# Placing the projection of a pair's gated half ahead of its recurrence

## The chip, the cores and the metric

The kernel runs on one core of a Trainium2 chip. The metric is the device time of one execution in microseconds (us), as the median of several runs. Engine names are those of the profile: PE is TensorE's matmul, PEld its weight load, DVE is VectorE, ACT is ScalarE, POOL is GpSimd, SP is SyncE, which here only issues DMAs.

## The reference, cut to what matters

One layer of a hybrid decoder over 544 tokens: 512 of a prompt and 8 sequences of 4 sample tokens. The part around the change:

```python
xn = rms_norm(x, norm1_g)
proj = xn @ w_in                              # 2048 -> 5 * 1024 + 288 columns
z_a = gelu(proj[..., :2 * W_A])               # u and v of the gated half, 1024 columns each
y_a = u * (spatial mixing of layer_norm(v))   # group A
y_b = rwkv7_mix(proj[..., 2 * W_A:], ...)     # group B: r, k, v, a recurrence over time per head
h = x + concat([y_a, y_b]) @ w_out
```

After it come the expert retrieval (`peer_ffn`) and a final norm, which take the larger part of the time and which the change doesn't touch.

## The kernel before, in words

Everything is kept transposed: a tile has 128 features as partitions and the tokens along its free axis. `front` computes the layer up to the gated half's share of the output projection, `back` the rest. All projections are float32 products done as three matmuls on split operands (`hi*xh + hi*xl + lo*xh`).

`project` (L160) computes one tile of 128 columns of `w_in` for all 552 token columns: two halves of 276 columns, each 16 x 3 = 48 matmuls (L171) into a PSUM tile of pool `pg` (two buffers). Its weights come through `weights` (L148): four DMAs of 256 KB into `wr` (four buffers), a cast on ACT (L155, `wh`) and a difference on DVE (L156, `wl`), in pools of seven buffers.

After the `v` side of the gated half, whose mixed result goes to a DRAM scratch `mix`, and three projections for the low-rank parts, a loop over eight pairs of heads (L544) does for pair p:

- `shifted` (L242) three times, for r, k and v: a projection, its eviction on DVE (L249) into a tile `p` (two buffers), and the token shift on DVE (L251, L252, L254) into a tile `r`, `k` or `v` (two buffers each).
- a DMA of the pair's low-rank weights `lora` (L547), and `seg` (L280) three times: tokens 0 to 255, 256 to 511, and the sample tokens. A `seg` begins with a chain over ACT, DVE and POOL from its first products (L300, L301 on `xwa` and `lora`, L323 on the squares of the scaled k) to the matrices `AR`, `BK`, `E`, goes on to a triangular inverse by doubling (L419, L434 to L441), and ends with the chunk recurrence (L466 to L501) and a normalisation (L508 to L525) whose result goes to the scratch `yT` rows 8 to 15. The second `seg` needs the state of the first.
- `utile` (L529): one more projection, for u of the gated half. Its two halves are evicted on DVE (L535) into a tile `p`, go through Gelu on ACT (L536), are multiplied with the mixed tile `mxr` (loaded by L538, one buffer; L539, L541), and go to `yT` rows 0 to 7 (L542). Nothing in it reads what a `seg` wrote, and no `seg` reads what it wrote.

After the loop `xns.close()` gives the memory of the projections' operands `xh`, `xl` free, and the stage `ya`, whose tiles take that memory, loads `yT` rows 0 to 7 (L559), splits them (L560, L561 into `yh`, `yl`) and multiplies them with the upper half of `w_out`: 16 x 48 = 768 matmuls (L573). When the pools of `front` close, `back` begins with the lower half of `w_out` (L675).

The order of the work on each engine is not written by hand. A planner runs when the program is built: it keeps its own model of when instructions become ready, and for each engine takes, among those ready in its model, the one with the lowest number in program order. `tc.high_priority(offset=n)` lowers the number by n (3000 for the weights, 2000 for the evictions). The order found is then fixed, and each engine runs its queue in that order. So work later in the program is placed into an engine's gaps of work earlier in the program.

Of the kernel before, what the change touches and what calls it, by code (L numbers as in the profile page):

```python
# [67 lines left out]
def front(tc, I, O, SC, dbg=None):  # L68
# [13 lines left out]
    def P(n, i=0, w=1):  # L82
        o = _PAR[n] + i
        return par[:, o:o + w]
# [75 lines left out]
    def project(ti, M=128, pool=None):  # L160
        pool, tag = pool or (pg, "g")
        ws = [weights(I["w_in"][ti], 4 * q, 4) for q in range(4)]
        out = []
        for h in range(2):
            ps = pool.tile([128, 512], F32, name=tag)
            c = slice(h * HC, h * HC + HC)
            n = 0
            for k in range(KT):
                hi, lo = (w[:, k % 4, :M] for w in ws[k // 4])
                for a, b in ((hi, xh), (hi, xl), (lo, xh)):  # L170
                    T.matmul(ps[:M, :HC], a, b[:, k, c], start=n == 0, stop=n == 3 * KT - 1)  # L171
                    n += 1
            out.append(ps[:M, :HC])
        return out
# [67 lines left out]
    def shifted(ti, n, name, M=128, bufs=None):  # L242

        ps = project(ti, M)
        p = b0.tile([128, CW], F32, name="p", bufs=2)
        for h in range(2):
            c = slice(h * HC, h * HC + HC)
            with tc.high_priority(offset=EV):
                V.tensor_mul(p[:M, c], ps[h], rs[:M, c])  # L249
        d = b0.tile([128, CW], F32, name="d")  # L250
        V.tensor_sub(d[:M, 1:], p[:M, :CW - 1], p[:M, 1:])  # L251
        V.tensor_scalar(d[:M, 0:1], p[:M, 0:1], -1.0, None, op0=OP.mult)  # L252
        q = b0.tile([128, CW], F32, name=name, bufs=bufs)
        V.scalar_tensor_tensor(q[:M], d[:M], P("mu", n)[:M], p[:M], op0=OP.mult, op1=OP.add)  # L254
        return q
# [273 lines left out]
    def utile(h):  # L529
        ps = project(h)  # L530
        u = b0.tile([128, CW], F32, name="p", bufs=2)
        for i in range(2):
            c = slice(i * HC, i * HC + HC)
            with tc.high_priority(offset=EV):
                V.tensor_mul(u[:, c], ps[i], rs[:, c])  # L535
            A.activation(u[:, c], u[:, c], AF.Gelu)  # L536
        mx = bw.tile([128, TC], F32, name="mxr")
        S.dma_start(mx, SC["mix"][h])  # L538
        V.tensor_mul(mx[:, :TP], mx[:, :TP], u[:, :TP])  # L539
        ms = mx[:, TP:].rearrange("p (b t) -> p b t", t=4)  # L540
        V.tensor_mul(ms, ms, u[:, TP:].rearrange("p (b t) -> p b t", t=5)[:, :, 1:])  # L541
        G.dma_start(SC["yT"][h], mx)  # L542

    for p in range(NPAIR):  # L544
        q = [shifted(16 + 8 * i + p, 8 * i + p, "rkv"[i], bufs=2) for i in range(3)]
        lora = bw.tile([128, 4, 128], F32, name="lora", bufs=2)
        S.dma_start(lora, I["lora"][p])  # L547
        st = seg(p, 0, q, lora, None)
        st = seg(p, 1, q, lora, st)
        seg(p, 2, q, lora, None)  # L550
        utile(p)
    xns.close()

    with tc.tile_pool(name="ya", bufs=1, side="right", reuse_waits="tile") as ya:
# [577 lines left out]
def emit(tc, I, O):  # L1132
    with tc.tile_pool(name="dram", bufs=1, space=DRAM) as dr:
        SC = scratch(dr)
        front(tc, I, O, SC)
        back(tc, I, O, SC)
# [87 lines left out]
```

## Time and profile before

| | |
|---|---|
| median of 3 runs | 4056.84 us (4054.25 to 4058.28) |
| the profiled execution | 4046.83 us, its span 4044.7 us |
| PE busy in the span | 3632.6 us, 90% |
| PEld, DVE, ACT, POOL busy | 84%, 76%, 35%, 32% |
| mean granted TensorE clock | 0.958 of 2.4 GHz |
| the pair loop | from about 235 to about 1063 us of the span |
| the stage `ya` | its matmuls from 993 to 1143 us, beside the last pair up to 1063 us |

Matmuls overlap in the array, and a row's duration is that of one from its start to its modelled end; the distance between starts in an unbroken stream is what one costs. Busy time of PE is therefore near 100% wherever matmuls follow one another closely, whatever their kind.

### The profile page before, as it was taken

What the parts mean: (1) busy time and instruction counts of PE and PEld (TensorE: products, weight loads), DVE (VectorE), ACT (ScalarE), POOL (GpSimd) and SP (SyncE); (2) the same over time, 40 slices, a digit from 0 to 9 for tenths busy, and PEclk for the clock granted to TensorE, in tenths of its full rate; (3) what the DMA queues carried; (4) which work ended last, traced back from release to release, by engine and by line L of the source; (5) the groups of instructions that cost most, each with busy time, mean ns of one, the idle gap of its engine ahead of it and who ended that gap; (6) DMA issues with size and microseconds to landing.
All of it is one profiled execution on the core that took longest, in us unless ns stands there. A gap on an engine that the chain in (4) does not pass through costs nothing.

```text
span 4044.7 us, 65633 instructions
## 1 busy us (share of the span) xinstructions
PE 3632.6 (90%) x25519; PEld 3413.5 (84%) x25519; DVE 3084.6 (76%) x5034; ACT 1425.5 (35%) x2501; POOL 1282.9 (32%) x1190
## 2 busy tenths in 40 slices
PE   8999999999999998889988888888988888898997
PEld 8888888887898997889888778887978788888997
DVE  4566666666645579999957888888898888888995
ACT  4244444444333232227942222222222222223233
POOL 1212222222143002221134443444434443444453
PEclk9999999999999999999999989999999998999998
DMA  4211111112554236667677898889889888998983
GB/s 156 102 62 56 58 59 57 59 57 78 178 170 120 75 115 234 235 225 260 252 242 287 311 341 310 318 310 341 317 326 325 317 322 305 333 331 311 358 332 123
DMA packets 252822, 886.53 MB, mean 219 GB/s; under 512 B 26920, under 2 KB 84008, under 8 KB 200480
## 3 DMA queue, kind: packets, MB, share of 16 engines
q1 hardware_dynamic: 184672, 423.77, 31.5%
q0 software_dynamic: 67840, 458.57, 30.3%
q8 instruction: 201, 3.29, 0.3%
q14 instruction: 109, 0.89, 0.1%
HBM read 823.47 MB, written 58.76 MB: 218 GB/s over the span
## 4 chain that ended last, share of the span: by engine, by line
PE 47%; DVE 16%; issue 15%; DMA 12%; POOL 8%; ACT 1%; SPq 0%; DVEq 0%; POOLq 0%; ACTq 0%
PE g L171 10%; PE o L1071 9%; PE g L675 9%; DMA row<-in_v_tab,idx 4%; PE q L970 4%; DVE wl L662 4%; DMA row<-in_u_tab,idx 3%; POOL row L807 3%; PE i L419 2%; DVE row L819 2%; DMA wr<-in_vT 2%; PE g L573 2%; POOL ac L1055 2%; POOL cl L1059 2%; DMA wr<-in_uT 1%
## 5 line engine op out<-in xcount | busy, mean ns | idle before, releaser
L661 ACT CAST wh<-wr 128x1024 fp32r<-128x1024 f32 x560 | 585.7, 1049 | 1441.4 <-PE o L1071 540.5
L662 DVE TENSOR_TENSOR wl<-wr,wh 128x1024 fp32r<-128x1024 f32 x560 | 730.3, 1308 | 205.2 <-ACT wh L661 200.4
L1071 PE MATMUL o<-ch,wh 128*128 128x352 f32 x2048 | 688.3, 343 | 190.1 <-DVE y L1079 146.8
L675 PE MATMUL g<-xh,wh 128*128 128x352 f32 x2048 | 678.3, 331 | 70.0 <-DVE ac L768 59.0
L1071 PE MATMUL o<-cl,wh 128*128 128x352 f32 x2048 | 695.0, 340 | 41.7 <-POOL cl L1059 41.7
L1071 PE MATMUL o<-ch,wl 128*128 128x352 f32 x2048 | 687.2, 337 | 0.7 <-DVE wl L662 0.7
L675 PE MATMUL g<-xh,wl 128*128 128x352 f32 x2048 | 672.9, 329 | 3.5 <-DVE wl L662 3.5
L675 PE MATMUL g<-xl,wh 128*128 128x352 f32 x2048 | 671.8, 328 | 0.0
L1071 PEld LDWEIGHTS o<-ch,wh 128*128 128x128 f32 x2048 | 407.5, 200 | 218.1 <-DVE y L1079 80.5
L819 DVE SCALAR_TENSOR_TENSOR row<-row,xrow 128x2048 f32<-128x2048 f32 x192 | 457.2, 2382 | 92.1 <-DMA row<-in_u_tab,idx 90.8
L838 DVE SCALAR_TENSOR_TENSOR acc<-row,dots,acc 128x2048 f32<-128x2048 f32 x186 | 458.8, 2467 | 63.7 <-DMA row<-in_v_tab,idx 61.6
L807 POOL DMA_INDIRECT row<-in_u_tab,idx x192 | 291.0, 1516 | 618.1 <-DVE y L1079 259.1
L675 PEld LDWEIGHTS g<-xh,wh 128*128 128x128 f32 x2048 | 391.4, 191 | 81.8 <-issue 40.9
L1071 PEld LDWEIGHTS o<-cl,wh 128*128 128x128 f32 x2048 | 411.2, 201 | 49.2 <-POOL cl L1059 49.0
L807 POOL DMA_INDIRECT row<-in_v_tab,idx x192 | 264.7, 1379 | 572.1 <-DVE y L1079 341.6
L1071 PEld LDWEIGHTS o<-ch,wl 128*128 128x128 f32 x2048 | 409.8, 200 | 1.0 <-DVE wl L662 1.0
L675 PEld LDWEIGHTS g<-xh,wl 128*128 128x128 f32 x2048 | 392.0, 191 | 5.6 <-DVE wl L662 5.4
L675 PEld LDWEIGHTS g<-xl,wh 128*128 128x128 f32 x2048 | 393.0, 192 | 1.0 <-issue 1.0
L171 PE MATMUL g<-xh,wh 128*128 128x276 f32 x1248 | 379.3, 304 | 9.6 <-ACT xh L113 9.6
L171 PE MATMUL g<-xl,wh 128*128 128x276 f32 x1248 | 375.9, 301 | 0.2 <-DVE xl L114 0.2
L171 PE MATMUL g<-xh,wl 128*128 128x276 f32 x1248 | 374.6, 300 | 0.0
L1079 DVE TENSOR_TENSOR y<-o,y 128x352 f32<-128x352 f32 x496 | 238.7, 513 | 36.0 <-PE o L1071 36.0
(636 smaller groups left out, 6378.6 us busy)
## 6 DMA issues: line engine op xcount, KB each, us to landing
wr<-in_uT SPq DMA_DIRECT2D x256, 512.0 KB
wr<-in_vT SPq DMA_DIRECT2D x256, 512.0 KB
wr<-in_w_in SPq DMA_DIRECT2D x172, 256.0 KB
Gd<-st POOLq DMA_DIRECT2D x11, 2048.0 KB
gl<-Gd SPq DMA_DIRECT2D x32, 704.0 KB
wr<-in_w_q SPq DMA_DIRECT2D x32, 512.0 KB
Cd<-ac POOLq DMA_DIRECT2D x52, 176.0 KB
ac<-Cd SPq DMA_DIRECT2D x52, 176.0 KB
```

The costliest lines, as they stand in the source:

```text
L171: T.matmul(ps[:M, :HC], a, b[:, k, c], start=n == 0, stop=n == 3 * KT - 1)
L419: return halves(lambda o, c, h: T.matmul(o, a[hs[h], c], b[hs[h], c], start=True, stop=True))
L573: T.matmul(ps[:, :TC // 2], a, b[:, k, h * TC // 2:(h + 1) * TC // 2], start=n == 0, stop=n == 23)
L661: A.copy(hi, raw)
L662: V.tensor_sub(lo, raw, hi)
L675: T.matmul(ps[:, :N], a, b[:, k, c], start=n == 0, stop=n == 3 * KT - 1)
L807: d = G.indirect_dma_start(out=u, out_offset=None, in_=tab, in_offset=bass.IndirectOffsetOnAxis(ap=idx[w][:, r:r + 1], axis=0))
L819: i = V.scalar_tensor_tensor(u, u, 1.0, xrow, op0=OP.mult, op1=OP.mult, accum_out=dots[w][:, r:r + 1])
L838: i = V.scalar_tensor_tensor(acc, u, dots[w][:, r:r + 1], acc, op0=OP.mult, op1=OP.add)
L970: T.matmul(ps[c][:, :TQ], w[:, j:j + 128], x, **e)
L1071: T.matmul(ps[j][:, :TD], a, x_, start=i + n == 0, stop=i == GB - 1 and n == 2)
L1079: last = V.tensor_add(yT[:, m], ps[j][:, :TD], prev)
```

## The change

In the loop over the pairs, the call of `utile(p)` moves from behind the three calls of `seg` to a place between the `shifted` calls and the load of `lora`. No instruction is added or removed; their numbers in program order change, and with them what the planner may put ahead of what.

```diff
     for p in range(NPAIR):
         q = [shifted(16 + 8 * i + p, 8 * i + p, "rkv"[i], bufs=2) for i in range(3)]
+        utile(p)
         lora = bw.tile([128, 4, 128], F32, name="lora", bufs=2)
         S.dma_start(lora, I["lora"][p])
         st = seg(p, 0, q, lora, None)
         st = seg(p, 1, q, lora, st)
         seg(p, 2, q, lora, None)
-        utile(p)
     xns.close()
```

## Rows read from the trace of the kernel before

**Rows 1.** From the page: busy tenths of PE and granted clock in 40 slices of 101 us each.

```profile
PE   8999999999999998889988888888988888898997
PEclk9999999999999999999999989999999998999998
```

**Rows 2.** Busy time in stretches of 104.2 us, one pair each (start and end, length; then the busy us and count of instructions of PE, PEld, DVE, ACT, POOL; the granted clock; DMA share, GB/s).

```profile
342.50:446.70 104.20, 101.84 (x1044) 86.79 (x1042) 71.19 (x191) 46.22 (x107) 23.58 (x43) 1.00 0.17 58
655.10:759.30 104.20, 101.80 (x1044) 86.77 (x1042) 71.17 (x191) 46.20 (x107) 23.58 (x43) 1.00 0.17 58
863.50:967.70 104.20, 101.80 (x1043) 86.77 (x1043) 71.15 (x191) 46.22 (x107) 23.60 (x44) 1.00 0.17 55
```

**Rows 3.** The stretches of one pair's period, all work; columns as in rows 2.

```profile
645.40:651.70 6.30, 6.30 (x51) 6.30 (x51) 3.81 (x10) 2.15 (x4) 1.08 (x2) 1.00 0.54 174
651.70:677.00 25.30, 22.93 (x220) 20.30 (x218) 19.36 (x39) 19.77 (x40) 9.45 (x15) 1.00 0.18 62
677.00:699.70 22.70, 22.70 (x311) 19.16 (x306) 15.19 (x49) 10.40 (x28) 8.17 (x14) 1.00 0.13 40
699.70:745.40 45.70, 45.67 (x455) 38.38 (x452) 30.88 (x90) 13.67 (x34) 4.90 (x12) 1.00 0.15 52
```

**Rows 4.** The same stretches, the projections' matmuls (L171) alone: busy us and count of PE and PEld, clock, DMA.

```profile
645.40:651.70 6.30, 6.30 (x50) 6.26 (x50) 1.00 0.54 174
651.70:677.00 25.30, 14.76 (x100) 12.86 (x98) 1.00 0.18 62
677.00:699.70 22.70, 9.98 (x55) 7.58 (x55) 1.00 0.13 40
699.70:745.40 45.70, 29.36 (x172) 23.21 (x172) 1.00 0.15 52
```

**Rows 5.** The timeline of PE in an unbroken stretch of projection (start us, duration, operation).

```profile
646.24 0.29 PE L171 MATMUL g<-xh,wl 128*128 128x276 f32 x1
646.37 0.29 PE L171 MATMUL g<-xh,wh 128*128 128x276 f32 x1
646.50 0.29 PE L171 MATMUL g<-xl,wh 128*128 128x276 f32 x1
```

**Rows 6.** Who PE waited for from 651.7 to 677 us (us in total, times, longest us).

```profile
PE q L379 <- DVE BK L350: 1.0, 1, 1.0
PE i L419 <- DVE Ti L429: 0.6, 1, 0.6
PE i L419 <- DVE Ti L438: 0.6, 1, 0.6
PE q L402 <- DVE E L393: 0.2, 1, 0.2
```

**Rows 7.** The timeline at the start of a pair's first `seg`: ACT, and below the line of dots DVE; in brackets the idle time before and its releaser.

```profile
651.80 0.62 ACT L155 CAST wh<-wr 128x512 fp32r<-128x512 f32 x1 [0.91 <-PE g L171]
652.44 1.28 ACT L303 ACT_TABLE_LOAD   x1
653.73 0.47 ACT L303 ACTIVATE sw<-q,hb 128x256 f32<-128x256 f32 x1
660.74 1.28 ACT L536 ACT_TABLE_LOAD   x1
662.03 0.43 ACT L536 ACTIVATE p<-p 128x276 f32<-128x276 f32 x1
666.69 0.47 ACT L303 ACTIVATE sw<-q,hb 128x256 f32<-128x256 f32 x1 [0.37 <-PE q L301]
...
651.93 0.44 DVE L249 TENSOR_TENSOR p<-g,rs 128x276 f32<-128x276 f32 x1 [0.31 <-PE g L171]
653.06 0.72 DVE L251 TENSOR_TENSOR d<-p 128x551 f32<-128x551 f32 x1
654.04 0.78 DVE L254 SCALAR_TENSOR_TENSOR v<-d,par,p 128x552 f32<-128x552 f32 x1
654.74 0.28 DVE L306 TENSOR_SCALAR sw<-sw 128x256 f32<-128x256 f32 x1
```

**Rows 8.** The line of the load of `mxr` in one period, on the SP queue: its wait (an event) and the DMA (count, duration in ns as minimum, median and maximum, first and last start).

```profile
L538 SPq EVENT_SEMAPHORE  x1: 6592/6592/6592, 678.0 to 678.0; - x1
L538 SPq DMA_DIRECT2D mxr<-mix x1: 327/327/327, 684.6 to 684.6; - x1
```

**Rows 9.** The last pair and the stage `ya`: stretches, all work; columns as in rows 2.

```profile
964.40:976.60 12.20, 11.16 (x87) 10.44 (x86) 8.45 (x17) 11.41 (x24) 3.20 (x6) 1.00 0.20 64
976.60:988.70 12.10, 10.78 (x118) 9.02 (x115) 9.98 (x21) 7.62 (x14) 6.21 (x8) 1.00 0.17 46
988.70:1001.50 12.80, 9.59 (x130) 7.61 (x128) 8.93 (x19) 7.98 (x20) 3.03 (x5) 0.87 0.68 216
1021.50:1063.00 41.50, 40.90 (x366) 32.64 (x367) 27.19 (x82) 9.01 (x24) 5.11 (x12) 1.00 0.28 81
1105.00:1143.60 38.60, 38.60 (x309) 38.60 (x309) 11.02 (x27) 4.34 (x7) 3.23 (x6) 1.00 0.43 139
```

**Rows 10.** The matmuls of `ya` (L573) alone in the stretches of the last pair: busy us and count of PE and PEld, clock, DMA.

```profile
988.70:1001.50 12.80, 1.19 (x5) 0.72 (x5) 0.87 0.68 216
1001.50:1021.50 20.00, 9.12 (x39) 5.75 (x39) 1.00 0.20 57
1021.50:1063.00 41.50, 23.35 (x134) 18.17 (x135) 1.00 0.28 81
```

**Rows 11.** The timeline around the first work of `ya`: the last matmul on `xh` and `xl`, the first load of `yT`, the first matmul of `ya`, the last split of its operand.

```profile
988.69 0.29 PE L171 MATMUL g<-xh,wl 128*128 128x276 f32 x1
988.88 0.33 SPq L559 DMA_DIRECT2D yr<-yT  x1
992.96 0.39 PE L573 MATMUL g<-yh,wh 128*128 128x272 f32 x1 [1.22 <-ACT yh L560]
1021.56 0.71 DVE L561 TENSOR_TENSOR yl<-yr,yh 128x544 fp32r<-128x544 f32 x1
```

## The prediction, made before the change was run

> **What bounds the kernel now.** I read the page's slices first [rows 1]: PE is busy in 80 to 90% of every slice and its clock is near full, so the loop over the pairs (about 235 to 1063 us) is to be read as work on PE. The second view is busy time by period [rows 2]: the reader is to see that each pair takes the same 104.2 us, that PE is busy for 101.8 of them, and that DVE (71), ACT (46) and POOL (24) are not near. PE's true idle time is only 104.2 - 101.8 = 2.4 us in a pair. The third view cuts one period into stretches and counts the projections' matmuls in each [rows 3, 4]. From 645.4 to 651.7 us PE does 50 of them and nothing else: the recurrence of the previous pair is over, and that of this one cannot start, since its v is still being projected. From 651.7 to 677 us the first `seg` of the pair goes through its chain on ACT, DVE and POOL, and 100 projection matmuls fill PE beside it. These are the pair's own `utile` (96 matmuls), the only projection that stands next in program order, and a few more. From 677 to 745.4 us the inverse and the recurrence have PE's gaps, and 55 + 172 projection matmuls of the next pair go into them. Then PE is alone with the rest of that pair's v again.
>
> A projection matmul costs 0.127 us in an unbroken stream [rows 5], so a projection of 96 costs 12.2 us, and the four of a pair 48.7 us: half of the period. The other half is the small matmuls and the switching between the two kinds. The short stretch in which PE does projections alone says that the filler is never used up within a pair: the recurrence hides what it can, and 6.3 us stay over.
>
> **The change part by part.** Nothing is added or removed; four things move.
>
> First, the order of the projections. Before it is r, k, v, [seg], u, r, k, v, [seg], u. After it is r, k, v, u, [seg], r, k, v, u, [seg]. The chain of projections is the same, and between two recurrences there are still four of them: u of this pair and r, k, v of the next before, r, k, v and u of the next after. `seg` keeps its precedence over all of those behind it. As filler one matmul is worth another, and I find no resource that would keep u of the next pair out of the gaps: it needs a `pg` and a `p` buffer, which turn over at each eviction, and weights, which come in the same order as before. So I expect the 50 lone matmuls to become matmuls of u instead of v, and the period to stay. Cost: 0, covered by the other pair's recurrence. If that cover were gone, all of u would stand alone, 12.2 us in each pair (a rival below).
>
> Second, what goes ahead of a `seg`'s chain on DVE and ACT. Before, the eviction and shift of v (0.44 + 0.72 + 0.78 us on DVE) and the table load for Tanh (1.28 us) stand between the last projection matmul at 651.7 and the chain; L303 starts 2.0 us behind it [rows 7]. After, v is long done, and the eviction (0.44) and Gelu (0.43) of u's second half stand there. Gelu and this Tanh do not need separate loads: behind a Gelu the Tanh at 666.69 started without one [rows 7]. So L303 could start some 0.23 + 0.44 + 0.43 + 0.1 = 1.2 us behind the last matmul, 0.8 earlier. This can only take from the 2.4 us of waits in that stretch [rows 6], which begin with 1.0 us before L379. The bounds: 2.4 us gained in a pair, if all of the waits go; 0.8 us lost, if Gelu's table load lands in front of the chain (1.28 less 0.44). I take a quarter of the 0.8, 0.2 us gained, because the order on PE was fixed by a model which will also see the chain begin earlier and put fewer matmuls ahead of L379. Eight pairs: -1.6 us (bounds -19 and +6).
>
> On what is left to gain the Trainium skill speaks in "Perfetto Trace Analysis", section Identifying the Most-Contended Engine: matmul busy time is no good measure of how close TensorE is to its limit, weight-load busy time is better. Here weight loads fill 86.8 of 104.2 us of a pair, against 6.30 of 6.30 in the lone stretch [rows 2, 3]; by that measure 17 us of a pair are in play and not 2.4. I don't price these 17: they are the changeovers between small and large matmuls, and their number goes with the gaps of the recurrence, which the change leaves.
>
> Third, DMAs and queues. u's load of `mxr` waits at the head of the SP queue for the single buffer, 6.6 us in a pair [rows 8], and the weight loads and `lora` wait behind it. It will still do so once in a pair, about 12 us earlier or later against the recurrence. The store L542 on POOL goes with it. PE never waits for weights in this stretch [rows 6], since up to seven buffers stand ready. Cost 0; if weights did run out, it would be up to those 6.6 us in a pair, which I hold for unlikely with DMA at 17% [rows 2].
>
> Fourth, the last pair, where the symmetry ends. Before, u of pair 7 is the filler of the last chain (964.4 to 988.7 us); with its last matmul the memory is free, the loads of `ya` start 0.2 us later, and its first matmul comes 4.3 us after that [rows 11]. After, u comes before the chain, ends 12.2 us behind v, and the last `seg` starts that much later with only `ya` as filler. The 12.2 us of u in front are compensated by the 12.2 us no longer spent in the chain only as far as `ya` fills the hole. `ya` ramps slowly, because its operand is split at low precedence: in the first 33 us only 5 + 39 of its matmuls run, 5.6 us [rows 10, 11]. I let the same 44 run in the new hole: 12.2 - 5.6 = 6.6 us stay open. Against it, the operand of `ya` is then complete about when the recurrence proper begins, and the 12.80 - 9.59 = 3.2 us of idle PE that the start of `ya` causes now [rows 9] go. Together +3.4 us. Bounds: if nothing fills the hole and the clock falls as it does at the start of `ya` now, 12.2 + 1.7 = +13.9; if the hole is filled and idle time and clock are both gained, -4.9. The 1.7: a clock of 0.87 over 12.8 us [rows 9] is 3.3 us at 1.2 GHz, in which half the work is lost. Behind this, `ya` runs alone until 1143 us [rows 9], so a delay or a gain up to there goes to the end in full, and `seg` itself, over at 1063, has 80 us to spare.
>
> The sum: 0 - 1.6 + 0 + 3.4 = +1.8 us. On the profiled execution's 4046.83 us that is 4048.6; the median of the runs lies 10 us higher (0.25%), so I add to the median: 4056.84 + 1.8 = 4058.6 us. What this kernel's measurement can tell from no change is about 0.2%, 8 us.
>
> **The rivals.** *Faster: the chain becomes shorter.* If the waits of the chain vanish in most pairs, the gain is 1.2 to 2.4 us in each, 10 to 19 us, and with the last pair at its sum 4041 to 4050 us. For it: the ACT queue is the fullest there (19.8 of 25.3 us, [rows 3]), and two table loads of u leave it. It decides from 1.5 us in a pair. Against: the order on PE is fixed beforehand. The Trainium skill, "ScalarE: Activation LUTs", section What ACT_TABLE_LOAD costs, would make this larger: 1.28 us of load and 1.38 us of drain for each switch. The trace shows the 1.28 and no drain behind it: the Gelu starts 0.01 us after its load [rows 7], so the measured price stands.
>
> *Slower: the hole in the last pair stays open.* +9 to +14 us, 4066 to 4071 us. For it: the slow ramp of `ya` and a granted clock that already falls to 0.87 there. It decides where less than a quarter of the hole is filled and the idle time at `ya`'s start returns. The Trainium skill, "TensorE: Matmul & The Clock Gate", part 1, names the mechanism: the slow clock is the default and activity releases it. The stretch from 988.7 us, PE idle for 3.2 us, agrees [rows 9].
>
> *Slower in every pair: u stands alone.* If the planner does not reach u of the next pair while the recurrence has gaps (a `p` buffer held while L538 waits, for instance), u costs its 12.2 us in each of seven pairs: +85 us, 4142 us. A twelfth of that would already show. Against it: 227 matmuls go into 677 to 745.4 us now, across three projections and their buffers [rows 4].
>
> **How the numbers follow.** Forecast within 8 us of before: 0.52. Shorter chain: 0.20. Hole in the last pair: 0.20. u alone, in whole or part: 0.08. So faster 0.20, same 0.52, slower 0.28. The range reaches from the middle of the faster rival's (4040) to past the hole with some loss in the pairs added (4056.84 + 13.9 + 6 = 4077, to 4080); the +85 is left out.
>
> **What would show it.** Right: periods of 103.5 to 104.7 us, with about 50 lone matmuls of u ahead of L300 and r and k of the next pair as filler of the chain; L303 without a table load; the last u ending some 12 us before its old distance to the end of the last `seg`; PE idle for 5 to 9 us more in the 25 us behind it. Wrong: a period that moves by more than 1 us, a lone stretch much above 6 us, PE waiting for `wl` or `wh`, or a stage behind 1143 us whose length changes by itself.

## The result, and the profile after

The changed kernel takes 4090.29 us (median of 4 runs, 4087.22 to 4102.47), the kernel before 4057.56 us beside it. The ratio is 1.0087, with a 95% interval of 1.0066 to 1.0109: slower, by 33 us where 2 were forecast, and above the range, which ended at 4080 us. The profiled execution is the slowest of the four (4102.47 us, span 4100.8), and that of before lay 10 us under its median, so the two profiles stand further apart (55.6 us) than the medians. 8 us of this lie ahead of the pair loop, in code that is the same in both: the first L300 comes at 254.7 us after 234.6 before, and only 12.2 us of that are the u which now stands in front. A kernel below with the same start of the loop reaches that L300 at 247.5 us, so these 8 us are spread between executions.

The first page line to look at is that of the slices. They tell nothing here, since PE looks as busy as before [rows 1]:

```profile
PE   8899999999899998889988788888888887989997
PEclk9999999999899999999999999999999999899998
```

The loss shows as soon as busy time is cut by period, as in [rows 2] (start and end, length; then busy us and count of PE, PEld, DVE, ACT, POOL; granted clock; DMA share, GB/s). A pair takes 109.20 us where it took 104.2, and each pair is like the next. The instructions are the same but for table loads on ACT, 9 in a pair where there were 11:

```profile
345.50:454.70 109.20, 105.18 (x1048) 88.35 (x1045) 73.27 (x191) 43.99 (x104) 23.70 (x42) 1.00 0.16 55
563.20:672.40 109.20, 105.18 (x1044) 88.36 (x1043) 73.26 (x190) 43.99 (x104) 23.71 (x42) 1.00 0.16 55
672.40:781.60 109.20, 105.18 (x1044) 88.35 (x1043) 73.28 (x190) 43.99 (x104) 23.71 (x42) 1.00 0.17 55
```

Seven periods of 5.0 us make 35 us, the whole loss of the median. PE's busy time grew from 101.8 to 105.2 us for the same matmuls, at full clock, so it counts waits too: a wait shorter than the modelled tail of the matmul ahead of it is not seen as idle. Weight-load busy time grew by 1.6 us only; by it 20.85 us of a pair are open (without a weight load) now, after 17.42.

So the cut has to follow the work. These are the stretches of one pair, the projections' matmuls (L171) alone (columns: PE, PEld, clock, DMA; a matmul that lies across a border is counted on both sides, so the sums below go by starts). They run from the first L300 to the first L379, to the first L469 (the recurrence begins), to the first L451 (the third `seg`'s state), to the last L519, and to the next L300. First the kernel before:

```profile
651.70:661.80 10.10, 8.01 (x59) 7.40 (x57) 1.00 0.22 76
661.80:688.90 27.10, 11.43 (x70) 9.35 (x70) 1.00 0.19 62
688.90:737.90 49.00, 29.13 (x164) 22.27 (x163) 1.00 0.13 42
737.90:749.30 11.40, 7.18 (x44) 5.87 (x44) 1.00 0.10 36
749.30:755.90 6.60, 6.40 (x50) 6.41 (x50) 1.00 0.49 168
```

and the changed kernel:

```profile
693.60:705.40 11.80, 9.04 (x70) 8.67 (x68) 1.00 0.29 102
705.40:732.70 27.30, 9.05 (x52) 7.12 (x52) 1.00 0.12 41
732.70:781.50 48.80, 26.98 (x145) 19.91 (x144) 1.00 0.10 32
781.50:794.40 12.90, 8.70 (x56) 7.40 (x56) 1.00 0.21 71
794.40:802.80 8.40, 8.16 (x64) 8.16 (x64) 1.00 0.43 134
```

The second and third stretch, the inverse and the recurrence, last 76.1 us in both. In them stand 70 + 163 = 233 projection matmuls before and 52 + 144 = 196 after. 37 fewer at 0.127 us are 4.7 us of projection that these 76 us no longer take in. They stand in the other three stretches instead: 11 ahead of L379, 12 behind L451, 14 alone in front of the next L300. Those three are 1.7, 1.5 and 1.8 us longer, together 5.0.

The first of the three has a cause that the profile names. The ACT queue from the start of a pair (start us, duration, line, operation; lines left out are marked). In the kernel before, whose pair starts at 651.73, the square root comes first, then the exponentials, then the copies of v into `SV`; the last line is DVE's, the step that the first L379 waits for:

```profile
655.88 0.42 ACT L325 ACTIVATE sq<-sq 128x256 f32<-128x256 f32 x1
...
657.61 0.42 ACT L312 ACTIVATE Pe<-cs 128x256 f32<-128x256 f32 x1
...
658.67 0.20 ACT L371 COPY SV<-q 64x64 f32<-64x64 f32 x1
...
661.33 0.41 DVE L350 TENSOR_TENSOR BK<-kk,iP 128x256 f32<-128x256 f32 x1
```

In the changed kernel, whose pair starts at 693.61, the copies come first and the square root last:

```profile
694.67 0.47 ACT L303 ACTIVATE sw<-q,hb 128x256 f32<-128x256 f32 x1
695.05 0.47 ACT L305 ACTIVATE a<-q,hb 128x256 f32<-128x256 f32 x1
695.54 0.20 ACT L371 COPY SV<-q 64x64 f32<-64x64 f32 x1
...
697.07 0.21 ACT L372 COPY SV<-q 64x64 f32<-64x64 f32 x1
697.29 1.28 ACT L312 ACT_TABLE_LOAD   x1
698.59 0.42 ACT L312 ACTIVATE Pe<-cs 128x256 f32<-128x256 f32 x1
698.91 0.40 ACT L314 ACTIVATE iP<-cs 128x256 f32<-128x256 f32 x1
699.22 0.40 ACT L316 ACTIVATE sw<-sw 128x256 f32<-128x256 f32 x1
699.62 1.28 ACT L325 ACT_TABLE_LOAD   x1
700.91 0.42 ACT L325 ACTIVATE sq<-sq 128x256 f32<-128x256 f32 x1
```

L303 starts 1.06 us behind the first L300 at 693.61 (2.0 us before), without a table load, as forecast. But v is ready by then, so its eight copies into `SV` (L371, L372) are ready too, and they stand ahead of the exponentials, and these ahead of the square root L325. The square root starts 7.3 us behind the start of the pair, after 4.15 us before (655.88 from 651.73). The reciprocal L326 on DVE (1.75 us), L327 on POOL and L350 hang on it one behind the other, and L379 on L350. Of the 3.15 us, 1.8 reach L379: before, DVE came to the reciprocal only 1.2 us after the square root's end (657.53 after 656.30), now at once (701.37 after 701.33). PE's waits say the same, against the 1.0 us of [rows 6]:

```profile
PE q L379 <- DVE BK L350: 1.9, 2, 1.5
PE i L419 <- DVE Ti L438: 0.9, 2, 0.6
PE i L419 <- DVE Ti L429: 0.6, 1, 0.6
```

In the last pair the hole is there. All work in its first 24 us, to be set against the first two lines of [rows 9]:

```profile
1021.20:1033.40 12.20, 4.17 (x18) 3.10 (x17) 8.86 (x18) 8.98 (x21) 3.06 (x4) 0.71 0.63 192
1033.40:1045.40 12.00, 10.74 (x98) 8.95 (x97) 7.29 (x17) 6.23 (x14) 4.81 (x7) 0.87 0.26 73
```

PE is busy for 14.9 of 24.2 us after 21.9 of 24.3, and the clock falls to 0.71 and 0.87. What it costs is told by experiments, since the clock differs from run to run there (0.67 to 0.75 in the first of the two stretches, over four kernels with u ahead of this pair).

### The profile page after: what moved, and what is told of

The parts are those of the page before. It is cut to its first block, busy times and chain, and to the rows that moved or that the text cites. A ratio compares the mean times of both kernels' runs of the same rounds, so it can differ in the third digit from the quotient of the medians.

```text
span 4100.8 us, 65665 instructions
## 1 busy us (share of the span) xinstructions
PE 3672.2 (90%) x25519; PEld 3438.0 (84%) x25519; DVE 3094.2 (75%) x5034; ACT 1408.6 (34%) x2487; POOL 1291.9 (32%) x1190
## 4 chain that ended last, share of the span: by engine, by line
PE 48%; DVE 17%; issue 13%; DMA 10%; POOL 9%; ACT 3%; DVEq 0%; SPq 0%; POOLq 0%; ACTq 0%
PE o L1071 11%; PE g L171 10%; PE g L675 9%; DVE wl L662 4%; PE q L970 4%; DMA row<-in_v_tab,idx 3%; DMA row<-in_u_tab,idx 3%; POOL row L807 3%; POOL ac L1055 2%; PE i L419 2%; DVE row L819 2%; PE g L573 2%; POOL cl L1059 2%; PE i L171 1%; PE qt L972 1%
## 5 line engine op out<-in xcount | busy, mean ns | idle before, releaser
L171 PE MATMUL g<-xh,wh 128*128 128x276 f32 x1248 | 377.3, 302 | 11.5 <-ACT xh L113 11.5
L171 PE MATMUL g<-xl,wh 128*128 128x276 f32 x1248 | 376.5, 302 | 0.2 <-DVE xl L114 0.2
L171 PE MATMUL g<-xh,wl 128*128 128x276 f32 x1248 | 373.5, 299 | 0.0
```

## The experiments

All kernels are named by the lines of the kernel before; where an edit shifts them, the same statement is meant, but lines of a profile keep the numbers of their own kernel. Times are medians, ratios are to the kernel before on the same chip, with the 95% interval. Stretches are those of the fences above, of a pair in the middle of the loop.

**Which part of the program loses.** Two kernels share the loop between the two orders. The first has u ahead in pairs 0 to 6 and behind in pair 7, the second has it ahead in pair 7 alone.

```diff
-        utile(p)
+        if p < NPAIR - 1:
+            utile(p)
...
         seg(p, 2, q, lora, None)
+        if p == NPAIR - 1:
+            utile(p)
```

The second kernel has the two conditions exchanged.

> u is ahead of the recurrence in pairs 0 to 6 and behind it in pair 7, as in the kernel before. If the hole in the last pair costs the 15 us that the two profiled executions show between the end of the last projection of v and the end of ya (182 us and 167 us, u's own 12.2 us set apart), the time is 4074 to 4080 us. If the whole loss is the seven periods of 109.2 instead of 104.2 us, it stays at 4085 to 4095 us.

> Only pair 7 has u ahead of its recurrence; pairs 0 to 6 are as in the kernel before. The hole alone: 4068 to 4074 us if it costs 11 to 16 us, 4056 to 4062 us if the earlier start of ya pays for it. Periods of pairs 0 to 6 of 104.2 us either way.

Measured: 4089.07 us, 1.0082 (1.0050 to 1.0114), period 109.2; and 4063.87 us, 1.0012 (0.9990 to 1.0033), period 104.2, between the two outcomes of its text. The loss is that of the seven periods. The last pair's hole is worth 5 us by the second ratio, with bounds of -4 and +13, so it can't be told from nothing.

**Is it the copies into SV?** Two edits of the changed kernel: v projected behind u (order r, k, u, v), so that v is late again; and the transposes and copies into `SV` moved as a block behind `E` and `R`.

```diff
-        q = [shifted(16 + 8 * i + p, 8 * i + p, "rkv"[i], bufs=2) for i in range(3)]
+        q = [shifted(16 + 8 * i + p, 8 * i + p, "rkv"[i], bufs=2) for i in range(2)]
         utile(p)
+        q.append(shifted(32 + p, 16 + p, "v", bufs=2))
```

```diff
-        SV = b2.tile([128, nch, 2, 64], F32, name="SV")
-        ps = pq.tile([128, 512], F32, name="q")
...
-                A.copy(SV[:64, c, 1], pv[lo:lo + 64, c // 2, 64:])
         BN = b2.tile([128, nch, 2, 64], F32, name="BN")
...
+        SV = b2.tile([128, nch, 2, 64], F32, name="SV")
+        ps = pq.tile([128, 512], F32, name="q")
...
+                A.copy(SV[:64, c, 1], pv[lo:lo + 64, c // 2, 64:])
```

> The projections of a pair come in the order r, k, u, v; u is still ahead of the recurrence, but v is the last before it, as in the kernel before. Theory A (v is too early: because v stands ready when the chain begins, its eight SV copies and the exponentials go ahead of the square root on ACT, and the chain up to the first L379 takes 11.9 us instead of 10.1): the square root is ahead of the exponentials again, the first L379 comes 10 us behind the first L300, the period is 104 to 105 us, and the time 4058 to 4072 us. Theory B (it is enough that u is ahead: the filler of the chain is then r and k of the next pair, and the recurrence lacks them): the period stays at 109 us and the time at 4085 to 4095 us.

> The changed kernel, and in addition the transposes of v and the SV copies stand later in a seg's program order, behind E and R. If the eight copies (1.75 us on ACT) ahead of the exponentials are what makes the chain late, the first L379 comes 10.1 to 10.6 us behind the first L300 instead of 11.85, and the period falls to 105 to 108 us. If the later square root is it (L325 behind the exponentials), L379 stays above 11 us and the period above 108 us.

Measured: v last, 4091.2 us, 1.0093 (1.0059 to 1.0126), L379 back at 10.08 us, but a period of 107.8, between those of the two theories. Copies late, 4062.61 us, 1.0021 (1.0003 to 1.0038), L379 at 10.2, periods of 104.1 and 106.3 in turn, 105.1 in the mean: 4.1 of the 5.0 us are back. In the pairs of 104.1 us ACT goes from the Tanh straight to the exponentials, and the square root stands 5.6 us behind the start of the pair (679.0):

```profile
680.48 0.47 ACT L305 ACTIVATE a<-q,hb 128x256 f32<-128x256 f32 x1
680.96 1.28 ACT L312 ACT_TABLE_LOAD   x1
...
683.30 1.28 ACT L325 ACT_TABLE_LOAD   x1
684.59 0.42 ACT L325 ACTIVATE sq<-sq 128x256 f32<-128x256 f32 x1
```

In the pairs of 106.3 us the square root stands ahead of the exponentials again, 4.5 us behind the start, and L379 comes no earlier (10.23). So that exponentials stand ahead of the square root does not make L379 late by itself; the 1.75 us of copies ahead of both are what makes L379 late. But the first of the two edits also says that the front of the chain alone is not the whole loss: with L379 as early as before, 3.6 us in a pair are still lost. There the inverse is 2.2 us shorter (24.9 after 27.1), the recurrence 3.4 longer (52.5 after 49.1) and the stretch behind it 2.5 longer (14.0 after 11.4).

**The same in doses, and in the other order.** The eight copies merged into four of twice the width, in the changed kernel and in that before; the copies late in the kernel before; and, in the kernel before, eight copies of 64x64 put between L305 and L312 for nothing but their time.

```diff
-            for c in range(nch):
-                lo = (c % 2) * 64
-                A.copy(SV[64 - 0:, c, 0], pv[lo:lo + 64, c // 2, :64])
-                A.copy(SV[:64, c, 1], pv[lo:lo + 64, c // 2, 64:])
+            for j in range(2):
+                A.copy(SV[64:, j::2, 0], pv[64 * j:64 * j + 64, :2, :64])
+                A.copy(SV[:64, j::2, 1], pv[64 * j:64 * j + 64, :2, 64:])
```

```diff
         Pe = new("Pe", 2)
+        if s == 0:
+            for j in range(8):
+                A.copy(Pe[:64, j % 4 * 64:j % 4 * 64 + 64], ps[:64, 256 + j % 4 * 64:320 + j % 4 * 64])
```

> The changed kernel, with the eight SV copies (0.22 us each on ACT) merged into four of twice the width; same place in the order. Theory (what ACT does between L305 and the exp of L312 delays L379): ACT has about half of the 1.75 us less there, first L379 0.6 to 0.9 us earlier than in the changed kernel (10.9 to 11.3 us behind L300) and the period 106 to 108 us, time 0.4 to 0.7% above before. Rival (the copies' time doesn't matter, only the place of the transposes on PE): period stays 109 to 109.5, time 0.7 to 1% above before.

> The kernel before with the same merged copies: does the edit gain by itself? Theory: the copies stand beside the chain here, not in front of it, so first L379 stays at 10.0 to 10.1 us behind L300, period 103.8 to 104.5, time within 0.2% of before. Rival (less work on ACT shortens the chain anyway): period 102.5 to 103.5, 0.2 to 0.4% faster. Second rival (the planner lays another order and it loses): period 105 to 108.

> The kernel before (u behind), with the SV transposes and their eight copies on ACT moved behind the matrices E and R in program order: the control of the same edit in the changed kernel. Theory (the copies harm only where v is ready early, and here they already stand behind the exp that L379 waits for): period 103.9 to 104.6 us, first L379 10.0 to 10.2 us behind L300, time within 0.2% of before. Rival (this edit gains in whichever order): period 102 to 103.5, time 0.3 to 0.5% below. Second rival (any reordering in seg costs a few us in a pair, as with the normalisation first): period 105.5 to 109, time 0.3 to 0.9% above.

> The kernel before (u behind), with eight copies of 64x64 on ACT put between L305 and the exp L312 of the first seg of each pair, written to a tile that the exp overwrites: they stand where the SV copies stand in the changed kernel. Is this delay enough by itself? Theory (1.75 us on ACT ahead of the exp delays L379, projections fill the wait, and the later stretches lose that fill at unchanged length): first L379 11.6 to 12 us behind L300, period 105.5 to 109.5 us, seven pairs and some +10 to +37 us, time 0.2 to 0.9% above before. Rival (the delay is harmless, the place of u is what costs): L379 late, but period 103.9 to 104.6 and the time within 0.2%.

Measured: merged in the changed kernel, L379 at 11.19 us (0.66 earlier) and a period of 108.54 (0.66 shorter), 1.0084 (1.0052 to 1.0116). The other stretches and the matmuls in them are those of the changed kernel, so this part of the loss goes one to one, and not further, as its theory had it (106 to 108); the time is too coarse to show 5 us. Merged in the kernel before: period 104.2, 0.9991 (0.9965 to 1.0017). Copies late in the kernel before: L379 unchanged at 10.08, yet a period of 107.15 and 1.0037 (1.0009 to 1.0066), the second rival of its text. The delay in the kernel before: L379 at 10.97 and a period of 107.15, 1.0021 (1.0001 to 1.0041). That delay is a smaller dose than was meant, since its eight copies took 0.95 us and not 1.75:

```profile
663.78 0.47 ACT L305 ACTIVATE a<-q,hb 128x256 f32<-128x256 f32 x1
664.14 0.95 ACT L314 COPY Pe<-q 64x64 f32<-64x64 f32 x8
665.56 0.42 ACT L317 ACTIVATE iP<-cs 128x256 f32<-128x256 f32 x1 [0.47 <-DVE cs L309]
...
667.92 0.42 ACT L328 ACTIVATE sq<-sq 128x256 f32<-128x256 f32 x1
```

Here L314 are the added copies, L317 an exponential and L328 the square root. The exponentials and the square root have changed places too, as in the changed kernel: the square root starts 6.5 us behind the start of the pair (661.40) and L379 is 0.9 us late. The pair loses 2.9 us: 0.9 up to L379, 0.5 from there to L451, 1.5 behind it. This doesn't show that the late front causes the rest, since the kernel before with the copies late loses the same 2.9 us with L379 on time. Its two stretches behind L451 (projections' matmuls, columns as above) are those of the changed kernel, with u in its old place:

```profile
754.05:767.00 12.95, 8.73 (x56) 7.42 (x56) 1.00 0.22 73
767.00:775.30 8.30, 8.16 (x64) 8.16 (x64) 1.00 0.44 149
```

So the 3.3 us that the changed kernel loses behind L451 need neither a late front nor the new place of u; an order that the planner made differently is enough.

**Other orders of the same work.** The normalisation of k (L319 to L327) ahead of the low-rank products, in the changed kernel and in that before; the difference L251 on POOL in place of DVE, in the changed kernel; u between the first and the second `seg`.

```diff
         r, k, v = (cols(t) for t in q)
+        kk = new("kk", 2)
+        A.activation(v3(kk), k, AF.Copy, scale=P("k_k", p))
...
+        G.tensor_mul(kk[:, :W], kk[:, :W], sq[:, :W])
         ps = pq.tile([128, 512], F32, name="q")
         T.matmul(ps[:, :W], lora[:, 0], cols(xwa), start=True, stop=True)
```

```diff
         st = seg(p, 0, q, lora, None)
+        utile(p)
         st = seg(p, 1, q, lora, st)
```

```diff
-        V.tensor_sub(d[:M, 1:], p[:M, :CW - 1], p[:M, 1:])
+        G.tensor_sub(d[:M, 1:], p[:M, :CW - 1], p[:M, 1:])
```

> The changed kernel, and in addition the normalisation of kk (from L319 to L327, with the square root) stands ahead of the low-rank products and exponentials in a seg's program order. Theory A (order on ACT): the square root comes ahead of the exponentials, the first L379 at most 10.5 us behind the first L300, the period falls by 2 to 5 us and the time to 4055 to 4076 us. Theory B (filler): the period stays within 1 us of 109.2 and the time at 4082 to 4095 us.

> A control: the kernel before with the normalisation of kk placed ahead of the low-rank products, the edit that took the changed kernel's period from 109.2 to 105.4 us. If that edit mends what the change broke (the order on ACT), it does nothing here, since the square root comes ahead of the exponentials already: period 103.9 to 104.5 us, time within 8 us of before. If it is a gain of its own, whatever the place of u, the period falls to 100 to 102 us and the time by 15 to 30 us.

> The changed kernel, and in addition the subtraction of the token shift (L251, 0.7 us on DVE, once in each projection of r, k, v) runs on POOL. If shifts and weight splits that stand on DVE between the steps of the chunk recurrence are what the recurrence lost (a step of 8.0 us where the kernel before has 5.1), the period falls by more than 1 us. If the order on PE alone is it, the period stays within 1 us of 109.2 us.

> u stands between the first and the second seg of its pair. u then fills the chain of the first seg as in the kernel before, since nothing else is ready there, and the first seg is served first. If what counts is only that u is not ahead of the first chain, the period is 103.5 to 105 us and the time within 8 us of before. If any earlier place of u costs, it lies between 104.2 and 109.2 us, the time 4070 to 4085 us.

Measured: 1.0032 (1.0008 to 1.0055) at a period of 105.4, as its first theory had it; 1.0075 (1.0050 to 1.0099) at 107.4 or 111.7; 1.0200 (1.0159 to 1.0241) at 112.7; 1.0094 (1.0057 to 1.0130) at 107 in the mean. The second was missed: with L379 half a microsecond earlier than before, at 9.57, the kernel before loses 3 us or more in a pair. The third was missed too, since neither of its two outcomes was a longer period. The fourth has its period where its second outcome put it, and a time above it. No order was measurably better than that of before.

**Are buffers what keeps the projections out?** Three buffers of `p` in place of two, which needs room, so `wh` and `wl` have six in place of seven; and the changed kernel with only the six.

```diff
-    wp = es.enter_context(tc.tile_pool(name="wp", bufs=7))
+    wp = es.enter_context(tc.tile_pool(name="wp", bufs=6))
-        p = b0.tile([128, CW], F32, name="p", bufs=2)
+        p = b0.tile([128, CW], F32, name="p", bufs=3)
```

> The changed kernel with three buffers of p in place of two; for the room, the pools of wh and wl have six buffers in place of seven. To be read against the next kernel, which has only the six. Theory (the planner's order, not buffers, keeps projection matmuls out of the stretches from the first L379 to L451): L379 to L451 holds 190 to 205 of them as in the changed kernel, period within 1 us of the next kernel's. Rival (p held until L541 or L254 is done stops the filler): 215 to 235 matmuls there, period 104 to 106.5, two or more us below the next kernel's.

> The changed kernel with six buffers of wh and wl in place of seven: the control of the kernel before it in this list. Theory: weights are never waited for, period 108.5 to 110, time 0.6 to 1.1% above the kernel before. Rival (weights are just enough at seven): period above 110.5, and PE waiting for wh or wl.

Measured: 1.0089 (1.0058 to 1.0120) and 1.0109 (1.0080 to 1.0138), both with a period of 109.2. From the first L379 to L451 the projections' matmuls are these, with three buffers of `p`:

```profile
699.50:775.50 76.00, 35.99 (x196) 26.97 (x196) 1.00 0.11 35
```

and with two:

```profile
699.50:775.50 76.00, 36.02 (x196) 26.99 (x196) 1.00 0.11 35
```

196 in both, to the matmul: neither a third `p` nor the seventh weight buffer makes a difference. The two buffers of `pg` were not varied. The trace speaks against them: in the changed kernel's 76 us there are eight gaps of over 0.33 us between starts on PE (three before), and in each the next projection matmul stands in the middle of the 48 that go into one `pg` tile, so that it had its buffer and its weights already.

**What bounds the pair.** Both orders with only the first of the three products in the loop's projections.

```diff
+                few = ti < 8 or 16 <= ti < 40
-                for a, b in ((hi, xh), (hi, xl), (lo, xh)):
+                for a, b in ((hi, xh), (hi, xl), (lo, xh))[:1 if few else 3]:
```

> The kernel before, with only the first of the three products (hi*xh) in the projections of the pair loop: 128 projection matmuls in a pair in place of 384, everything else kept (the weights' loads, casts and differences too). It leaves out part of the computation and its time is no gain. What does it show: whether the stretch from the first L379 to the first L451 of a pair (76.15 us, 233 projection matmuls, in the kernel before) is bound by PE or by the dependent chain through it. Theory (chain): 74 to 78 us with however few matmuls, and a period of 92 to 100 us. Rival (PE is the bound, as the prediction read it): 0.127 us less for each matmul that is missing; with 128 at most in it, at most 62.9 us, and a period near 104.2 - 256 x 0.127 = 71.8 us.

> The changed kernel with the same two thirds of the projections' matmuls left out of the pair loop. Theory (the dependent chain sets the pair, and the change lengthens its front by the SV copies ahead of the exp): the stretch from the first L379 to the first L451 again 74 to 78 us; first L379 1 to 2 us later behind L300 than in the same cut of the kernel before; period 1 to 3 us above its. Rival (the loss of 5.0 us in a pair comes from where the projection matmuls stand, so it goes when most are gone): period within 0.5 us of the cut kernel before.

Measured: 4015.9 us, 0.9900 (0.9814 to 0.9985), and 4015.98 us, 0.9909 (0.9862 to 0.9955). A period in the middle of the cut kernel before, and below it one of the cut changed kernel, all work:

```profile
554.40:660.30 105.90, 87.22 (x786) 67.57 (x785) 72.21 (x190) 48.34 (x108) 22.89 (x42) 0.76 0.18 57
```

```profile
553.90:660.10 106.20, 87.43 (x786) 67.83 (x785) 72.27 (x190) 48.38 (x108) 22.95 (x42) 0.76 0.19 56
```

256 matmuls fewer, and the pair takes no less than 104.2 us. Part of that is the clock, 0.76 here, 1.00 in [rows 2]; but even 105.9 x 0.76 = 80 us, an estimate as if all of the time went with the clock, are above the 71.8 of a pair bound by PE. These two pairs take the same and so do the kernels, as the rival of the second text had it (the loss goes with the projections' matmuls), and the delay of 1 to 2 us was not to be seen. But this settles neither: the next two pairs of the cut changed kernel take 109.0 and 109.4 us at clocks of 0.73 and 0.72, and in both kernels the planner let the next pair's chain overlap with this one's recurrence, where a late front need not show. For the same reason it failed as a test of the 76 us: the stretch (71.4 us) is not the same thing.

The stretches side by side (us; "matmuls" are the projections' that start in the stretch from L379 to L451; 384 in a pair). Where periods alternate, both are given.

| kernel | L300 to first L379 | first L379 to L451 | matmuls | period |
|---|---|---|---|---|
| before | 10.07 | 76.15 | 233 | 104.2 |
| before, SV merged | 10.1 | 76.13 | 233 | 104.2 |
| changed, SV late | 10.2 | 77.4 / 76.3 | 231 / 217 | 104.1 / 106.3 |
| changed, normalisation first | 9.6 | 75.1 | 220 | 105.4 |
| before, delay on ACT | 11.0 | 76.7 | 211 | 107.15 |
| before, SV late | 10.1 | 75.8 | 205 | 107.15 |
| v last | 10.1 | 77.4 | 215 | 107.8 |
| changed, SV merged | 11.2 | 76.1 | 196 | 108.5 |
| changed | 11.85 | 76.1 | 196 | 109.2 |
| before, normalisation first | 9.6 | 76.2 / 80.5 | 213 / 213 | 107.4 / 111.7 |
| u behind the first `seg` | 10.1 / 11.5 | 84.0 / 79.0 | 268 / 236 | 107.6 / 107.1 |
| changed, L251 on POOL | 11.9 | 79.6 | 196 | 112.7 |

Read down: in the first nine rows the stretch lasts 75 to 77.4 us, whether 196 or 233 matmuls are laid into it. So there its length follows the chain through it and not the number of PE's matmuls; with 268 it grows to 84 us. What is not laid into it is paid outside: before, 151 matmuls stand in the other 28.1 us, and those of the nine rows that have at least ten more there pay 0.11 to 0.17 us for each of them, near the 0.127 of a stream. The last three rows have longer stretches for reasons of their own that were not sought. Since the direct test was spoilt by the clock and by another order, this is a reading over many orders, not a proof by one.

## Why the prediction was wrong

**What bounds the kernel.** Here it went wrong first. PE's true idle time was put at 2.4 us in a pair, from busy time, and from this followed that PE's work fixes the period. The 68 us from 677 to 745.4 showed no idle time in [rows 3], and the prediction called them covered. They are the stretch in which 37 matmuls could be left out with no gain in length. Two of the prediction's own signs of being wrong came, a period that moved by more than 1 us and a lone stretch much above 6 us (8.4). The measure was even at hand: weight loads filled 86.8 of 104.2 us [rows 2]. The prediction named the 17 us that are left and declined to price them, as changeovers, which no run shows. The Trainium skill's "Perfetto Trace Analysis", section Identifying the Most-Contended Engine, prefers weight-load busy time to matmul busy time as the measure of TensorE. The trace of after agrees: weight loads fill 88.35 of 109.20 us, so 3.4 of the 5.0 us lie outside them. One reading was wrong besides: that the recurrence can't start while its v is projected. L300 and L301 read only `xwa` and `lora`, and in the changed kernel it is u, which no `seg` reads, that stands alone ahead of L300 in the same way. By the planner's rule it is their lower number in program order that puts the projections there.

**First step, the period stays: cost 0.** This is the step that failed, by 3.3 of the 5.0 us in each of seven pairs. Its structure came true: matmuls of u stand alone in front of L300, r and then k of the next pair fill the chain and the inverse. What failed is the cover: it was taken for granted that the planner would lay as many matmuls beside the recurrence as before. It laid 196 there and not 233, and 64 stood alone where about 50 were foreseen. That "as filler one matmul is worth another" is not refuted, since the kernel before with late copies has the same two stretches behind L451 with u in its old place. The rival of u alone saw the sign and the symptom but not the mechanism: +85 us was its price, 35 came, and u does reach the gaps (32 of its 96 matmuls).

**Second step, the chain starts 0.8 us earlier: -1.6 us.** This step failed too, by the rest. The start came true, L303 0.9 us earlier against the first L300 and without a load. The end of the chain did not: the first L379 came 1.8 us later. The step listed what left the front (v's eviction and shift on DVE, the load for Tanh on ACT) and u's eviction and Gelu, but not what else could now come in on ACT: the copies of v into `SV`, 1.75 us, ahead of the exponentials and the square root. Its bound for a loss, 0.8 us in a pair, was too small by 1.0. The merged copies show this term one to one, for 0.66 of the 1.8 us.

**Third step, DMAs and queues: 0.** The cost came true, the wait did not: L538 should have waited 6.6 us once in a pair as before, and its event lasts 17 ns in seven of the eight pairs. Weights were never waited for, not even with six buffers.

**Fourth step, the last pair: +3.4 us.** The hole is there: 7 us more of idle PE in the first 24 us, where 5 to 9 were foreseen, and a clock of 0.71. The kernel with u ahead in the last pair alone gives +5, with bounds of -4 and +13. Not shown wrong, and small beside the periods.

**What stays open.** That the copies ahead of the square root make the front 1.8 us longer is shown by the profile and by the merged copies. Why the planner lays 37 matmuls fewer into the 76 us is not, and with it the cause of the other 3.3 us stays open. Moving the copies away gave back 4.1 of 5.0 us, about 2.4 more than the front's part, but an edit of the order also has the planner lay everything anew: three orders with an L379 as early as before, or earlier, lose about 3 us or more too (v last, and the kernel before with late copies or with the normalisation first). A third `p` and the weights' buffers are excluded, `pg` only by the trace. The order is one fixed beforehand by a model of the times, and where that model departs from the chip was not seen.

## What to carry to other kernels

Where queues are fixed beforehand, ask of a moved step which instructions it makes ready earlier, and on which in-order queue these then stand ahead of the chain: eight copies of 0.2 us made the chain's first matmul 1.8 us late here. Don't read a stretch as bound by an engine because its busy time is full; compare its length in two orders that put different amounts of filler in it, or look at the weight loads. And price a change of order itself: in this loop, orders of the same work gave pairs of 104.1 to 112.7 us, and none measurably faster than the first. An edit that puts one thing back is then no proof of what that thing cost, unless the rest of the order stays as it was, as with the merged copies.

## What the runs showed of the hardware

With two thirds of the projections' matmuls gone from the loop, the granted clock of TensorE fell from 1.00 to 0.76 in the middle of it (PE busy 87 of 106 us, after 102 of 104), that is, about halfway between 1.2 and 2.4 GHz, so that it stood at 1.2 GHz for about half of the time. Leaving out two thirds of these matmuls gained 1% of the kernel's time; how much of the rest the clock took and how much the new order was not separated.
